# Block products of 256 columns, gate and up tiles by halves, and fewer adding DMAs in an fp32 encoder of two layers

## The chip, the cores and the metric

The kernel runs on one core of a Trainium2 chip. The metric is the device time of one execution in microseconds (us). Engines are named as in the profile: PE (TensorE, matmuls), PEld (its weight loads), DVE (VectorE), ACT (ScalarE), POOL (GpSimd) and SP (SyncE, here only a queue of DMAs).

## The reference

Input is one sequence of 512 rows and 1024 channels in float32. Two layers follow each other, each with a SwiGLU network, a mixer and a second SwiGLU network, and all of it in float32:

```
def _rmsnorm(x, gain):
    xf = x.astype(jnp.float32)
    y = xf * lax.rsqrt(jnp.mean(xf * xf, axis=-1, keepdims=True) + EPS)
    return (y * gain.astype(jnp.float32)).astype(x.dtype)
def _swiglu(h, w_gate, w_up, w_down):
    return (jax.nn.silu(h @ w_gate) * (h @ w_up)) @ w_down

# every layer:
#   x += 1/2 * SwiGLU(RMSNorm(x))                       1024 -> 2816 -> 1024
#   x += W_out [mixer_1 || mixer_2] (split of W_in RMSNorm(x))
#   x += 1/2 * SwiGLU(RMSNorm(x))
# even layer: Mamba-2 SSD heads || S5 complex-diagonal groups
# odd layer:  chunked band attention || multi-scale causal pooling
```

## The kernel before

**Stages.** The program runs six stages one after another: f0, even, f1 (layer 0) and f2, odd, f3 (layer 1). f0 to f3 are the SwiGLU networks, "even" and "odd" the mixers. x lies on the chip as eight tiles of 128 channels x 512 positions.

**Products.** An fp32 product is made of three matmuls (`mm3`): high part of the weights by high part of the data, high by low, low by high. So every weight unit (`raw`, 128 x 1024, by DMA) is split into `whl`: ACT casts it to the high part, DVE subtracts to get the low part (`split`). Units listed in `BY_DMA` take another way (`split_dma`): ACT writes the negated cast into the low part, a DMA of POOL adds the weights to it from memory, and ACT casts them into the high part; DVE does nothing.

**SwiGLU.** Gates and ups come in 11 pairs of 128-column tiles. The first pairs (`CLASSIC`: eight in f0, two in f1, f2, f3) are plain products of 512 columns (`proj_tile`); DVE multiplies them by the norm's factors rsB into `gs` and `us` (`evac`). The others, three pairs in f0 and nine in each of f1, f2, f3, gate and up each, 60 in all, go through `pair`: seven block products instead of eight, by sums of weights and of data (a scheme of Strassen's kind), into accumulators X, Y, Z on PE, which DVE adds up into `gs` or `us` (`plus`, `add`, `times`; p1 and p5 are small tiles). A `block` is four steps over 128 channels. A narrow block has three matmuls of 256 columns at each step. A wide one (three of the seven, where `WIDE`) puts the high weights against high and low data in one matmul of 512 columns, so that two halves of the accumulator must be added by DVE afterwards. `gate` takes silu of `gs` on ACT, multiplies by `us` on DVE, and splits the product into two `hg` tiles. Between the pairs stand units of the product with w_down (`out_unit`).

**Norms.** `norm` makes h from x as soon as a tile of x is final: ACT writes x times gain as the high part hg, DVE the low part. `norm_factors` squares each x tile on ACT (`sq`), DVE adds it to `acc`, PE multiplies by ones, DVE finds the inverse root (rqv, rqt, rqy), PE spreads it (ident, rqy) and ACT copies it to rsB.

**Even mixer.** Its small jobs are products with parameters of the S5 part (`prm`, eight matrices of 1 MB that a DMA loads), the products of the SSD part, the norm of its output (ysq) and transposes. Rows of the S5 part go through memory: us is stored as s5us and loaded again as hg, ys is stored as s5ys and loaded as yv.

**What sets the order.** PE, DVE and ACT run instructions in the order in which the builder writes them. A planner (`Clock`) holds an estimated time for each engine; the small jobs are generators that are advanced when the planner's clock says that their inputs are ready, `SLACK` later by stage, while the big products go on. It knows the Rings (`raw`, `whl`, `hg`), but not the waits for a buffer of an ordinary pool, such as `sq`:

```
                sq = self.rsp.tile([P, S], F32, tag="sq", name=self.n("sq"), bufs=2)
                nc.scalar.activation(out=sq, in_=x, func=AF.Square)
                yield from self.on("DVE", sq)
                nc.vector.tensor_tensor(out=acc, in0=acc, in1=sq, op=ALU.add)
```

Of the kernel before, what the change touches and what calls it, by code (L numbers as in the profile page):

```python
# [8 lines left out]
F32 = mybir.dt.float32  # L9
# [3 lines left out]
ALU = mybir.AluOpType  # L13
# [4 lines left out]
P = 128  # L18
# [23 lines left out]
CLASSIC = (2, 8)  # L42
LEAD = (0, 0)

WIDE = (True, True)

# [4 lines left out]
GUARD = {"f0": 2.5, "even": 1.5, "f1": 1.5, "f2": 1.5, "odd": 2.0, "f3": 1.5}  # L51
BY_DMA = {"wgu1": (1, 4), "wgu2": (1, 4), "wgu3": (1, 4), "wev": (13, 16), "wglu": (0, 2), "wevo": (0, 1), "wod": (8, 16), "wodo": (0, 1)}
LOADS = (1, 4)
LAG = 4
WARM = 12
SLACK = {"f0": 1.5, "even": 0.0, "f1": 0.0, "f2": 0.0, "odd": 0.4, "f3": 0.0}
PREP_SLACK = 4.0
# [53 lines left out]
class Clock:  # L111


    def __init__(self):
        self.t = dict.fromkeys(list(ENGINES.values()) + ["RING", "DMA"], 0.0)
        self.t["ACT"], self.t["RING"], self.t["DVE"], self.t["PE"] = 1.9, 0.65, 0.6, 0.95
        self.w, self.r, self.floor, self.stuck = {}, {}, 0.0, 0
        self.reads, self.writes, self.fine = {}, {}, True
        self.lanes, self.born = [0.0] * 8, {}
# [53 lines left out]
    def note(self, eng, op, args, kw):  # L173
# [14 lines left out]
        if dma and eng == "POOL":  # L188
            self.t["POOL"] = max(at, self.t["POOL"]) + 1.1
            end = max(self.t["DMA"], self.t["POOL"] + 1.0) + max(0.18, out.free_size() * out.partition_size() * 4 / 360e3)  # L190
            self.t["DMA"] = end
            end += 0.95
        elif dma:
            at = max(at, self.lanes.pop(0))
            self.t["RING"] = at + 0.48
            end = max(self.t["DMA"], at + 1.1) + max(0.06, out.free_size() * out.partition_size() * 4 / 360e3)
            self.t["DMA"] = end
            end += 1.06
            self.lanes.append(end)
        else:  # L200
            end = at + self.cost(eng, op, out, kw)
            if eng == "DVE" and self.fine:
                end += self.moved([ap for ap in ins if ap.free_size() > 1], out)
                if op == "reciprocal":
                    end += out.free_size() * 0.005
            self.t[eng] = end
# [61 lines left out]
class Builder:  # L268
# [27 lines left out]
    def phase(self, name):  # L296
        self.name = name
        self.clk.fine = name == "f0"
        self.backlog, self.guard, self.most = BACKLOG[name], GUARD[name], AHEAD[name]
# [352 lines left out]
    def norm_factors(self, h):  # L652
        nc = self.nc
        acc = None
        for k in range(KD):
# [4 lines left out]
            if acc is None:  # L660
                acc = self.rsp.tile([P, S], F32, tag="acc", name=self.n("acc"))
                nc.scalar.activation(out=acc, in_=x, func=AF.Square)
            else:
                sq = self.rsp.tile([P, S], F32, tag="sq", name=self.n("sq"), bufs=2)
                nc.scalar.activation(out=sq, in_=x, func=AF.Square)
                yield from self.on("DVE", sq)
                nc.vector.tensor_tensor(out=acc, in0=acc, in1=sq, op=ALU.add)
# [98 lines left out]
    def ffn(self, f, gi, then, prepare=None):  # L766
# [4 lines left out]
        with ExitStack() as st:  # L771
# [18 lines left out]
            for key in ffn_items(f):  # L790
# [11 lines left out]
                if key[0] == "wgu":  # L802
                    m, i = key[2:]
                    if (m % 2, i) == (0, 0):
                        t, done = {"gs": None, "us": None}, []
                    if (m, i) == (0, 0):
# [3 lines left out]
                    else:  # L810
                        w = self.unit(*key)
                        ps = self.proj_tile(w, h)
                        self.give(w)
                    self.add("evac", self.evac(ps, t, "us" if i else "gs", m % 2, done))
                    if (m % 2, i) == (1, 1):
                        self.add("gate", self.gate(t, g, m // 2, done, 0))
                        if m == NFF - 1:
                            self.give(*h)
                elif key[0] == "pair":
                    q, i = key[2:]  # L820
                    if i == 0:
                        t = {}
                    last = self.pair(w, t, "us" if i else "gs", pending)

                    def pending(last=last, t=t, q=q, i=i):
                        last()
                        if i == 0:
                            nc.scalar.activation(out=t["gs"], in_=t["gs"], func=AF.Silu)
                        else:
                            self.add("gate", self.gate(t, g, q, [1] * 4, 1))  # L830
                            if q == NFF // 2 - 1:
                                self.give(*self.N, *self.TS)
                else:
# [21 lines left out]
    def tail(self):  # L855
        self.final, self.xdone = True, [False] * KD
        if self.then is not None:
            self.start_norm(self.then)

    def ftile(self, tag):  # L860
        self.wait_room(tag, 1)
        return self.ft.tile([P, 2, S], F32, tag=tag, name=self.n(tag), bufs=1)

    def evac(self, ps, t, tag, m, done):
        while not self.scaled():
            yield
        while t[tag] is None and self.cnt.get(tag, 0):
            yield
        if t[tag] is None:
            self.cnt[tag] = 1  # L870
            t[tag] = self.ft.tile([P, 2, S], F32, tag=tag, name=self.n(tag), bufs=1)
        yield from self.on("DVE", ps, self.rsB)
        self.evac_rs(ps, t[tag][:, m])
        self.free(ps)
        done.append(1)

# [66 lines left out]

    def pair(self, w, t, tag, before):
        v = self.nc.vector
# [17 lines left out]
        if before:  # L963
            Z = self.main_ps()
            self.block(Z[:, hi], W4, 512, N[4:8], hi)
            before()
        t[tag] = dst = self.ftile(tag)
        Y = self.main_ps()
        self.block(Y, W3, 512, TA, 1, wide=wide)
        plus(dst[:, 0, hi], Y, p1)  # L970
        if not before:
# [4 lines left out]

        add(dst[:, 0, hi], Z[:, lo], dst[:, 0, hi])
        p5 = new("p5", 1)
        times(p5, Z[:, hi], hi)
        add(dst[:, 0, hi], dst[:, 0, hi], p5)  # L980
        self.block(X, W1, 512, N[4:8], lo, more=True)
        self.give(W1)
        times(dst[:, 0, lo], X[:, lo], lo)
        self.free(X)
        self.block(Y, W4, 0, TB, 0, more=True, wide=wide)
        self.give(W4)
        plus(dst[:, 1, hi], Y, p1)
# [1128 lines left out]
```

## Time and profile before

| | |
|---|---|
| three timed runs | 1807.51, 1810.75, 1813.69 us; median 1810.75 |
| profiled execution | 1812.46 us, of which the traced span is 1810.8 |
| granted TensorE clock, mean | 0.998 |
| PE busy | 1787.6 us (99%), 10082 matmuls |
| DVE busy | 1518.0 us (84%), 2902 instructions |
| ACT busy | 744.5 us (41%), 1032 |
| POOL busy | 33.9 us (2%) |
| DMA | 216.57 MB, mean 120 GB/s |
| the norms' products with ones, one at each stage's start | f0 21.2, even 384.9, f1 590.4, f2 937.9, odd 1284.3, f3 1466.3 us |

An engine's busy time is the union of its instructions' spans. A timeline row holds a start, a length, the engine, the line, the operation with its output and inputs (buffer numbers left out), the shape and how many instructions were merged into it. A row of waits holds who waited for whom, then the total, the times and the longest in us. All instructions are recorded at one line (L223), so groups go by tile names.

### The profile page before, as it was taken

To read this page: it belongs to the slowest core of one execution; us is meant where nothing else is said; L and a number is where in the kernel's file an instruction comes from. 1 tells how busy PE (TensorE), PEld (TensorE's weight loads), DVE (VectorE), ACT (ScalarE), POOL (GpSimd) and SP (SyncE) were. 2 spreads that over 40 slices of the span, in tenths; PEclk is the share of its full clock that TensorE was granted. 3 is DMA by queue.
4 is the path that set the end of the run, shared out by engine and by line. 5 is a ranking of instruction groups with operands and counts; after the bars stand their busy time and mean duration, and the time that the engine had idled before them with its cause. 6 is when DMAs were issued, how large, how long until landed. Compare 5 with 4: busy or idle time off the path is not lost.

```text
span 1810.8 us, 26209 instructions
## 1 busy us (share of the span) xinstructions
PE 1787.6 (99%) x10082; PEld 1536.4 (85%) x10082; DVE 1518.0 (84%) x2902; ACT 744.5 (41%) x1032; POOL 33.9 (2%) x53
## 2 busy tenths in 40 slices
PE   9999999999999999999999999999999999999999
PEld 7876888878778889998888999988888888999987
DVE  8989888778885899998779998987678679998984
ACT  4323433333584543333354333333466554333331
POOL 0000000000010000000010000000000010000000
PEclk9999999999999999999999999999999999999999
DMA  5346533336674533333343333333325452333332
GB/s 193 101 130 173 165 93 94 124 133 197 170 180 131 126 105 105 105 104 106 128 114 107 105 106 105 103 108 116 111 82 114 132 128 86 112 105 95 115 98 77
DMA packets 83341, 216.57 MB, mean 120 GB/s; under 512 B 18288, under 2 KB 30608, under 8 KB 82064
## 3 DMA queue, kind: packets, MB, share of 16 engines
q1 hardware_dynamic: 78032, 196.52, 33.9%
q0 software_dynamic: 5040, 18.35, 5.9%
q8 instruction: 79, 1.29, 0.3%
q14 instruction: 46, 0.38, 0.1%
q10 hardware_dynamic: 144, 0.02, 0.0%
HBM read 202.26 MB, written 12.60 MB: 119 GB/s over the span
## 4 chain that ended last, share of the span: by engine, by line
PE 75%; DVE 15%; DMA 5%; issue 2%; ACT 2%; SPq 1%; DVEq 0%; ACTq 0%
PE ps L223 75%; DVE whl L223 3%; DMA raw<-in_wgu_dram 2%; DVE hg L223 2%; DVE raw L223 2%; DVE us L223 1%; ACT whl L223 1%; DVE gs L223 1%; SPq L223 1%; DVE ct L223 1%; DVE ex L223 1%; DMA prm<-ct 1%; DVE g L223 0%; DMA prm<-prm 0%; DMA raw<-in_wev_dram 0%
## 5 line engine op out<-in xcount | busy, mean ns | idle before, releaser
L223 PE MATMUL ps<-hg,whl 128*128 128x512 f32 (+1 forms) x8400 | 1593.3, 350 | 5.4 <-DVE gs L223 2.5
L223 PEld LDWEIGHTS ps<-hg,whl 128*128 128x128 f32 x8400 | 1341.5, 189 | 210.9 <-issue 7.7
L223 ACT CAST whl<-raw 128x1024 fp32r<-128x1024 f32 x374 | 390.4, 1047 | 437.3 <-PE ps L223 306.6
L223 DVE TENSOR_TENSOR whl<-raw,whl 128x1024 fp32r<-128x1024 f32 x339 | 412.1, 1218 | 81.0 <-ACT whl L223 80.6
L223 ACT CAST hg<-us 128x512 fp32r<-128x512 f32 x88 | 52.7, 618 | 209.0 <-DVE us L223 208.9
L223 DVE TENSOR_TENSOR raw<-raw,raw 128x512 f32<-128x512 f32 (+1 forms) x212 | 131.0, 646 | 2.5
L223 ACT ACTIVATE gs<-gs 128x1024 f32<-128x1024 f32 x44 | 46.7, 1060 | 155.0 <-DVE gs L223 154.9
L223 DVE SCALAR_TENSOR_TENSOR x<-ps,x 128x512 f32<-128x512 f32 x128 | 83.1, 683 | 23.9 <-PE ps L223 23.9
L223 PE MATMUL ps<-hg,wh 128*128 128x512 f32 x480 | 94.2, 339 | 1.1 <-DVE gs L223 1.1
L223 PEld LDWEIGHTS ps<-hg,wh 128*128 128x128 f32 x480 | 77.3, 189 | 13.9 <-DVE gs L223 1.7
L223 DVE TENSOR_TENSOR us<-ps,us 128x256 f32<-128x256 f32 x150 | 63.5, 424 | 22.2 <-PE ps L223 17.8
L223 DVE TENSOR_TENSOR raw<-raw 128x512 f32<-128x512 f32 (+1 forms) x92 | 54.5, 592 | 18.9 <-DMA raw<-in_wgu_dram 18.8
L223 DVE TENSOR_TENSOR gs<-ps,gs 128x256 f32<-128x256 f32 x150 | 63.6, 424 | 6.6 <-PE ps L223 1.0
L223 DVE TENSOR_TENSOR hg<-us,hg 128x512 fp32r<-128x512 f32 x88 | 58.4, 684 | 2.7 <-ACT hg L223 2.7
L223 DVE TENSOR_TENSOR us<-gs,us 128x1024 f32<-128x1024 f32 x44 | 53.7, 1220 | 0.4
L223 DVE TENSOR_TENSOR us<-ps,p 128x256 f32<-128x256 f32 x90 | 37.8, 419 | 16.1 <-PE ps L223 15.4
L223 DVE TENSOR_TENSOR p<-ps,rsB 128x256 f32<-128x256 f32 x120 | 49.9, 416 | 1.7 <-PE ps L223 1.7
L223 ACT ACTIVATE hg<-x,gains 128x512 fp32r<-128x512 f32 x48 | 33.5, 718 | 34.6 <-DVE x L223 32.1
L223 DVE TENSOR_TENSOR gs<-ps,p 128x256 f32<-128x256 f32 x90 | 37.8, 420 | 8.1 <-PE ps L223 6.3
L223 DVE TENSOR_TENSOR wh<-raw,wh 128x512 fp32r<-128x512 f32 x60 | 41.0, 684 | 0.0
L223 ACT ACTIVATE whl<-raw 128x1024 fp32r<-128x1024 f32 x35 | 36.9, 1056 | 8.1 <-PE ps L223 5.1
L223 DVE SCALAR_TENSOR_TENSOR hg<-x,gains,hg 128x512 fp32r<-128x512 f32 x48 | 35.3, 745 | 5.7 <-ACT hg L223 5.7
(258 smaller groups left out, 1084.2 us busy)
## 6 DMA issues: line engine op xcount, KB each, us to landing
raw<-in_wgu_dram SPq DMA_DIRECT2D x176, 512.0 KB, 3.5
raw<-in_wdn_dram SPq DMA_DIRECT2D x88, 512.0 KB, 4.1
whl<-in_wgu_dram POOLq DMA_DIRECT2D x18, 512.0 KB, 6.3
raw<-in_wev_dram SPq DMA_DIRECT2D x16, 512.0 KB, 4.2
prm<-prm SPq DMA_DIRECT2D x8, 1024.0 KB, 6.9
raw<-in_wod_dram SPq DMA_DIRECT2D x12, 512.0 KB, 3.5
raw<-in_wevo_dram SPq DMA_DIRECT2D x8, 512.0 KB, 6.4
raw<-in_wodo_dram SPq DMA_DIRECT2D x8, 512.0 KB, 6.4
```

The costliest lines, as they stand in the source:

```text
L223: r = f(*args, **kw)
```

## The change

1. `WIDE` becomes false for all stages: every block is narrow, and `plus` is one add.
2. `gs` and `us` were one tile of 128 x 2 x 512 each, of one buffer. They are now tiles of 128 x 512, three buffers of gs and two of us (`HALVES`). Silu, product and split are done for each half, as soon as it is complete (`ready`).
3. `BY_DMA` of the gate and up weights in f1, f2, f3 covers two pairs of 128-column tiles instead of three: m = 2 and 3, no longer 1. Six units fewer go by POOL's adding DMA (18 before, 12 after), and those are split by DVE.
4. `SLACK` of the even mixer is 0.5 where it was 0.
5. The planner reckons POOL's DMAs in f1, f2, f3 at 160 GB/s where it reckoned 360.
6. The tile `sq` has one buffer where it had two.

```diff
-
-WIDE = (True, True)
+HALVES = {"gs": 3, "us": 2}
+
+WIDE = (False, False)
...
-BY_DMA = {"wgu1": (1, 4), "wgu2": (1, 4), "wgu3": (1, 4), "wev": (13, 16), "wglu": (0, 2), "wevo": (0, 1), "wod": (8, 16), "wodo": (0, 1)}
+BY_DMA = {"wgu1": (2, 4), "wgu2": (2, 4), "wgu3": (2, 4), "wev": (13, 16), "wglu": (0, 2), "wevo": (0, 1), "wod": (8, 16), "wodo": (0, 1)}
-SLACK = {"f0": 1.5, "even": 0.0, "f1": 0.0, "f2": 0.0, "odd": 0.4, "f3": 0.0}
+SLACK = {"f0": 1.5, "even": 0.5, "f1": 0.0, "f2": 0.0, "odd": 0.4, "f3": 0.0}
...
-            end = max(self.t["DMA"], self.t["POOL"] + 1.0) + max(0.18, out.free_size() * out.partition_size() * 4 / 360e3)
+            end = max(self.t["DMA"], self.t["POOL"] + 1.0) + max(0.18, out.free_size() * out.partition_size() * 4 / (160e3 if self.ffn else 360e3))
...
-                sq = self.rsp.tile([P, S], F32, tag="sq", name=self.n("sq"), bufs=2)
+                sq = self.rsp.tile([P, S], F32, tag="sq", name=self.n("sq"), bufs=1)
...
                 elif key[0] == "pair":
                     q, i = key[2:]
                     if i == 0:
                         t = {}
-                    last = self.pair(w, t, "us" if i else "gs", pending)
-
-                    def pending(last=last, t=t, q=q, i=i):
+                    def ready(m, t=t, q=q, i=i):
+                        if i == 0:
+                            nc.scalar.activation(out=t["gs", m], in_=t["gs", m], func=AF.Silu)
+                        else:
+                            self.add("gate", self.gate(t, g, q, m, False))
+
+                    last = self.pair(w, t, "us" if i else "gs", pending, ready)
+
+                    def pending(last=last, q=q, i=i):
                         last()
-                        if i == 0:
-                            nc.scalar.activation(out=t["gs"], in_=t["gs"], func=AF.Silu)
-                        else:
-                            self.add("gate", self.gate(t, g, q, [1] * 4, 1))
-                            if q == NFF // 2 - 1:
-                                self.give(*self.N, *self.TS)
+                        if (q, i) == (NFF // 2 - 1, 1):
+                            self.give(*self.N, *self.TS)
...
     def ftile(self, tag):
-        self.wait_room(tag, 1)
-        return self.ft.tile([P, 2, S], F32, tag=tag, name=self.n(tag), bufs=1)
+        self.wait_room(tag, HALVES[tag])
+        return self.ft.tile([P, S], F32, tag=tag, name=self.n(tag), bufs=HALVES[tag])
...
-        t[tag] = dst = self.ftile(tag)
+        t[tag, 0] = d0 = self.ftile(tag)
         Y = self.main_ps()
         self.block(Y, W3, 512, TA, 1, wide=wide)
-        plus(dst[:, 0, hi], Y, p1)
+        plus(d0[:, hi], Y, p1)
         if not before:
             Z = self.main_ps()
             self.block(Z[:, hi], W4, 512, N[4:8], hi)
         self.block(Z, W3, 0, TA, 0)
         self.give(W3)
 
-        add(dst[:, 0, hi], Z[:, lo], dst[:, 0, hi])
+        add(d0[:, hi], Z[:, lo], d0[:, hi])
         p5 = new("p5", 1)
         times(p5, Z[:, hi], hi)
-        add(dst[:, 0, hi], dst[:, 0, hi], p5)
+        add(d0[:, hi], d0[:, hi], p5)
         self.block(X, W1, 512, N[4:8], lo, more=True)
         self.give(W1)
-        times(dst[:, 0, lo], X[:, lo], lo)
+        times(d0[:, lo], X[:, lo], lo)
         self.free(X)
+        ready(0)
+        t[tag, 1] = d1 = self.ftile(tag)
         self.block(Y, W4, 0, TB, 0, more=True, wide=wide)
         self.give(W4)
-        plus(dst[:, 1, hi], Y, p1)
-        add(dst[:, 1, hi], Z[:, lo], dst[:, 1, hi])
+        plus(d1[:, hi], Y, p1)
+        add(d1[:, hi], Z[:, lo], d1[:, hi])
         self.free(Z)
 
         def last():
             self.block(Y, W2, 0, TB, 1, more=True, wide=wide)
             self.give(W2)
-            plus(dst[:, 1, lo], Y, p1)
+            plus(d1[:, lo], Y, p1)
             self.free(Y)
+            ready(1)
         return last
...
-    def gate(self, t, g, q, ready, done):
+    def gate(self, t, g, q, m, silu):
         nc = self.nc
-        while len(ready) < 4:
-            yield
-        gs, us = t["gs"], t["us"]
-        if done < 1:
+        gs, us = t["gs", m], t["us", m]
+        if silu:
             yield from self.on("ACT", gs)
             nc.scalar.activation(out=gs, in_=gs, func=AF.Silu)
-        if done < 2:
-            yield from self.on("DVE", gs, us)
-            nc.vector.tensor_tensor(out=us, in0=gs, in1=us, op=ALU.mult)
+        yield from self.on("DVE", gs, us)
+        nc.vector.tensor_tensor(out=us, in0=gs, in1=us, op=ALU.mult)
         self.leave("gs")
-        for i in range(2):
-            o = yield from self.grab("hg")
-            yield from self.split_steps(us[:, i], o)
-            g[2 * q + i] = o
+        o = yield from self.grab("hg")
+        yield from self.split_steps(us, o)
+        g[2 * q + m] = o
         self.leave("us")
```

**What moves.** PE, a wide block of a pair in f0, before (Y, with the data sums hg and the weights whl; a step's three rows of work in two matmuls):

```order
L223 MATMUL ps_2573<-hg_2036,whl_2472 128x512 [waits Activation_49]
L223 MATMUL ps_2573<-hg_2036,whl_2472 128x256
L223 MATMUL ps_2573<-hg_2090,whl_2472 128x512
L223 MATMUL ps_2573<-hg_2090,whl_2472 128x256
L223 MATMUL ps_2573<-hg_2157,whl_2472 128x512
L223 MATMUL ps_2573<-hg_2157,whl_2472 128x256
L223 MATMUL ps_2573<-hg_2257,whl_2472 128x512
L223 MATMUL ps_2573<-hg_2257,whl_2472 128x256
```

and after:

```order
L224 MATMUL ps_2616<-hg_2066,whl_2507 128x256 [waits Activation_49]
L224 MATMUL ps_2616<-hg_2066,whl_2507 128x256 x2
L224 MATMUL ps_2616<-hg_2137,whl_2507 128x256 x3
L224 MATMUL ps_2616<-hg_2214,whl_2507 128x256 x3
L224 MATMUL ps_2616<-hg_2297,whl_2507 128x256 x3
```

Eight matmuls, four of them of 512 columns, are now twelve of 256; the places of the blocks in PE's order stay as they were.

ACT at the norm of f1, before (sq is the square of an x tile, hg the high part of x times gain, whl a weight unit; DVE_49 is a wait for DVE, DMAHW for a load):

```order
L223 ACTIVATE sq_5346<-x_123 128x512 [waits Activation_49]
L223 ACTIVATE sq_5376<-x_125 128x512 [waits DVE_49]
L223 ACTIVATE whl_5378<-raw_5257 128x1024 [waits DMAHW1_49]
L223 CAST whl_5378<-raw_5257 128x1024
L223 ACTIVATE hg_5374<-x_127,gains 128x512 [waits DVE_49]
L223 ACTIVATE whl_5395<-raw_5286 128x1024 [waits DMAHW2_49]
L223 CAST whl_5395<-raw_5286 128x1024
L223 ACTIVATE sq_5412<-x_127 128x512 [waits DVE_49]
L223 ACTIVATE whl_5417<-raw_5317 128x1024 [waits DMAHW3_49,PE_49]
```

and after:

```order
L224 ACTIVATE sq_5446<-x_123 128x512 [waits DVE_49]
L224 ACTIVATE sq_5476<-x_125 128x512 [waits DVE_49]
L224 CAST whl_5478<-raw_5357 128x1024 [waits DMAHW5_49,DMAHW1_49]
L224 ACTIVATE hg_5474<-x_127,gains 128x512
L224 CAST whl_5490<-raw_5386 128x1024 [waits DMAHW2_49]
L224 ACTIVATE whl_5502<-raw_5417 128x1024 [waits DMAHW3_49,PE_49]
L224 CAST whl_5502<-raw_5417 128x1024
L224 ACTIVATE sq_5516<-x_127 128x512 [waits DVE_49,Activation_49]
```

The squares sq_5446 (of x_123), sq_5476 (of x_125) and sq_5516 (of x_127) now wait for DVE's add of the square before, since they use its buffer. Two units (m = 1) that were negated and cast are only cast here, which leaves their subtraction to DVE, and the last square stands behind a third unit's negation and cast.

DVE at the same place, before:

```order
L223 TENSOR_TENSOR acc_5186<-acc_5186,sq_5333 128x512 [waits Activation_49]
L223 TENSOR_TENSOR x_127<-ps_5228,x_127 128x512 [waits PE_49]
L223 SCALAR_TENSOR_TENSOR hg_5340<-x_125,gains,hg_5340 128x512 [waits Activation_49]
L223 TENSOR_TENSOR acc_5186<-acc_5186,sq_5346 128x512 [waits DVE_49,Activation_49]
L223 TENSOR_TENSOR acc_5186<-acc_5186,sq_5376 128x512 [waits DVE_49,Activation_49]
L223 SCALAR_TENSOR_TENSOR hg_5374<-x_127,gains,hg_5374 128x512 [waits Activation_49]
L223 TENSOR_TENSOR acc_5186<-acc_5186,sq_5412 128x512 [waits DVE_49,Activation_49]
```

and after:

```order
L224 TENSOR_TENSOR acc_5286<-acc_5286,sq_5433 128x512 [waits Activation_49]
L224 TENSOR_TENSOR x_127<-ps_5328,x_127 128x512 [waits PE_49]
L224 SCALAR_TENSOR_TENSOR hg_5440<-x_125,gains,hg_5440 128x512 [waits Activation_49]
L224 TENSOR_TENSOR acc_5286<-acc_5286,sq_5446 128x512 [waits Activation_49]
L224 TENSOR_TENSOR whl_5478<-raw_5357,whl_5478 128x1024 [waits DMAHW2_49,DMAHW4_49,DMAHW1_49,Activation_49]
L224 TENSOR_TENSOR whl_5490<-raw_5386,whl_5490 128x1024 [waits DMAHW2_49,Activation_49]
L224 SCALAR_TENSOR_TENSOR hg_5474<-x_127,gains,hg_5474 128x512 [waits DVE_49]
L224 TENSOR_TENSOR acc_5286<-acc_5286,sq_5476 128x512 [waits DVE_49]
L224 TENSOR_TENSOR acc_5286<-acc_5286,sq_5516 128x512 [waits Activation_49]
```

The two subtractions (whl_5478, whl_5490) have come in ahead of the low half hg_5474 of the last x tile and of the last two adds.

SP's queue in the even mixer, before (s5us and s5ys are the rows that go through memory, yv and hg their loads, prm the parameters):

```order
L223 DMA s5ys_3999<-ys_3942 16x8x64 x8
L223 DMA s5us_3969<-us_3960 128x512
L223 DMA prm_4011<-prm_144 128x2048
L223 DMA prm_4077<-prm_145 128x2048
L223 DMA raw_4082<-in_wev_dram 128x1024
L223 DMA s5ys_4084<-ys_3990 16x8x64 x8
L223 DMA yv_4093<-s5ys_3999 128x512
L223 DMA hg_4101<-s5us_3969 16x16x64 x8
```

and after:

```order
L224 DMA s5ys_4090<-ys_4067 16x8x64 x8
L224 DMA s5us_4048<-us_4039 128x512
L224 DMA prm_4101<-prm_143 128x2048
L224 DMA prm_4121<-prm_144 128x2048
L224 DMA raw_4145<-in_wev_dram 128x1024
L224 DMA yv_4171<-s5ys_4090 128x512
L224 DMA hg_4177<-s5us_4048 16x16x64 x8
L224 DMA raw_4215<-in_wev_dram 128x1024
L224 DMA prm_4228<-prm_145 128x2048
L224 DMA s5ys_4233<-ys_4119 16x8x64 x8
```

The load of hg from s5us stood behind the second set of stores s5ys; it now stands ahead of it, behind the load of yv.

More of the change, by code (lines that the diff above doesn't have):

```diff
@@ L117, in __init__ @@
         self.w, self.r, self.floor, self.stuck = {}, {}, 0.0, 0
-        self.reads, self.writes, self.fine = {}, {}, True
+        self.reads, self.writes, self.fine, self.ffn = {}, {}, True, False
         self.lanes, self.born = [0.0] * 8, {}
@@ L297, in phase @@
         self.name = name
-        self.clk.fine = name == "f0"
+        self.clk.fine, self.clk.ffn = name == "f0", name in ("f1", "f2", "f3")
         self.backlog, self.guard, self.most = BACKLOG[name], GUARD[name], AHEAD[name]
@@ L804, in ffn @@
                     if (m % 2, i) == (0, 0):
-                        t, done = {"gs": None, "us": None}, []
+                        t = {}
                     if (m, i) == (0, 0):
@@ L813, in ffn @@
                         self.give(w)
[L814 to L818, printed above, removed]
+                    self.add("evac", self.evac(ps, t, "us" if i else "gs", m % 2, g, m // 2))
+                    if (m, i) == (NFF - 1, 1):
+                        self.give(*h)
                 elif key[0] == "pair":
@@ L860, in ftile, with evac @@
     def ftile(self, tag):
-        self.wait_room(tag, 1)
-        return self.ft.tile([P, 2, S], F32, tag=tag, name=self.n(tag), bufs=1)
-    def evac(self, ps, t, tag, m, done):
+        self.wait_room(tag, HALVES[tag])
+        return self.ft.tile([P, S], F32, tag=tag, name=self.n(tag), bufs=HALVES[tag])
+    def evac(self, ps, t, tag, m, g, q):
         while not self.scaled():
             yield
-        while t[tag] is None and self.cnt.get(tag, 0):
-            yield
-        if t[tag] is None:
-            self.cnt[tag] = 1
-            t[tag] = self.ft.tile([P, 2, S], F32, tag=tag, name=self.n(tag), bufs=1)
+        yield from self.room(tag, HALVES[tag])
+        o = self.ft.tile([P, S], F32, tag=tag, name=self.n(tag), bufs=HALVES[tag])
         yield from self.on("DVE", ps, self.rsB)
-        self.evac_rs(ps, t[tag][:, m])
+        self.evac_rs(ps, o)
         self.free(ps)
-        done.append(1)
+        t[tag, m] = o
+        if tag == "us":
+            self.add("gate", self.gate(t, g, q, m, True))
     def normed(self, r, k, h, gi, late):
@@ L940, in block, with pair @@
             self.tick()
-    def pair(self, w, t, tag, before):
+    def pair(self, w, t, tag, before, ready):
         v = self.nc.vector
@@ L993, in last @@
             self.give(W2)
-            plus(dst[:, 1, lo], Y, p1)
+            plus(d1[:, lo], Y, p1)
             self.free(Y)
+            ready(1)
         return last
-    def gate(self, t, g, q, ready, done):
+    def gate(self, t, g, q, m, silu):
         nc = self.nc
-        while len(ready) < 4:
-            yield
-        gs, us = t["gs"], t["us"]
-        if done < 1:
+        gs, us = t["gs", m], t["us", m]
+        if silu:
             yield from self.on("ACT", gs)
             nc.scalar.activation(out=gs, in_=gs, func=AF.Silu)
-        if done < 2:
-            yield from self.on("DVE", gs, us)
-            nc.vector.tensor_tensor(out=us, in0=gs, in1=us, op=ALU.mult)
+        yield from self.on("DVE", gs, us)
+        nc.vector.tensor_tensor(out=us, in0=gs, in1=us, op=ALU.mult)
         self.leave("gs")
-        for i in range(2):
-            o = yield from self.grab("hg")
-            yield from self.split_steps(us[:, i], o)
-            g[2 * q + i] = o
+        o = yield from self.grab("hg")
+        yield from self.split_steps(us, o)
+        g[2 * q + m] = o
         self.leave("us")
```

## The prediction, made before the changed kernel ran

> **What bounds the kernel now.** I read the page first: busy shares, then the clock row, then the list of PE's waits.
>
> ```profile
> PE 1787.6 (99%) x10082; PEld 1536.4 (85%) x10082; DVE 1518.0 (84%) x2902; ACT 744.5 (41%) x1032; POOL 33.9 (2%) x53
> PE 75%; DVE 15%; DMA 5%; issue 2%; ACT 2%; SPq 1%; DVEq 0%; ACTq 0%
> ```
>
> PE is busy 1787.6 of 1810.8 us. Only two things can move the time: the 1787.6 themselves, and the 23.2 us in which PE stands. The second line, the chain that ended last, says the same: three quarters PE. DVE has 16% to spare on the average, so work taken from DVE is worth only what PE waits for it.
>
> ```profile
> PE ps L223 <- DVE gs L223: 3.6, 7, 0.9
> PE ps L223 <- DVE bt L223: 2.7, 4, 1.2
> PE ps L223 <- DMA prm<-prm: 2.3, 1, 2.3
> PE ps L223 <- DMA hg<-s5us: 2.0, 1, 2.0
> PE ps L223 <- DVE hg L223: 1.6, 2, 1.2
> PE ps L223 <- ACT bl L223: 1.3, 1, 1.3
> PE ps L223 <- DVE ysq L223: 1.2, 1, 1.2
> PE ps L223 <- DVE cr L223: 0.9, 1, 0.9
> ```
>
> These are PE's waits (total, times, longest). The gs row is the first pair of f1, f2, f3; bt and bl are preparations in f0; prm, s5us, one hg of 1.2, ysq and cr are the even mixer. None is in the steady pairs.
>
> **Narrow blocks.** A pair's three wide blocks (4 matmuls of 512 columns and 4 of 256) become 12 matmuls of 256. The timeline of f2 has one of each, a wide one and then the next pair's first narrow one (start, length with the drain of the last matmul):
>
> ```profile
> 1104.57 1.56 PE L223 MATMUL ps<-hg,wh 128*128 128x512 f32 x8
> 1105.97 1.60 PE L223 MATMUL ps<-hg,whl 128*128 128x256 f32 x12
> ```
>
> 1.60 against 1.56 is 0.04 us a block; the wide one's 8 matmuls take 1.40 to the next start. There are 60 pairs, so 180 blocks: 180 x 0.04 = **+7.2 us**, all of it on PE. The two rows bound it closely, 6 to 8. The Trainium skill's "TensorE: Matmul & The Clock Gate", section "Back-to-back issue gap", has N/2.4 + 2.5 ns for a matmul of N columns, by which a split matmul costs only 2.5 ns more: 4 x 2.5 = 10 ns a block and +1.8 us in all. The trace's 40 ns disagree, and I keep them.
>
> **One add less, halves, fewer adding DMAs.**
>
> ```profile
> L223 DVE TENSOR_TENSOR us<-ps,us 128x256 f32<-128x256 f32 x150 | 63.5, 424 | 22.2 <-PE ps L223 17.8
> L223 DVE TENSOR_TENSOR us<-gs,us 128x1024 f32<-128x1024 f32 x44 | 53.7, 1220 | 0.4
> L223 DVE TENSOR_TENSOR acc<-acc,sq 128x512 f32<-128x512 f32 x42 | 28.8, 686 | 5.9 <-ACT sq L223 5.0
> L223 DVE TENSOR_TENSOR whl<-raw,whl 128x1024 fp32r<-128x1024 f32 x339 | 412.1, 1218 | 81.0 <-ACT whl L223 80.6
> ```
>
> 180 adds at 0.424 leave DVE (-76 us). Products by halves cost 88 x 0.686 - 44 x 1.220 = +7 us (taking the 512-column add's duration for a 512-column product), and six weight units that a POOL DMA finished are now split by DVE: 6 x 1.218 = +7. All this lies beside PE: the steady pairs wait for nothing, so I count 0. If that cover went, DVE being 84% busy, it would be a gain of DVE time, not a loss. ACT's silus by halves are 44 more small instructions on an engine at 41%: 0. POOL and its queue lose six DMAs: 0. The planner's price for these DMAs moves loads, not engine work.
>
> Where DVE is late, it matters: the first pairs of f1 to f3 stall for 3.5 us of the gs row. DVE there has one add less before the accumulators come free, and a gs half frees sooner. Between 0 and 3.5 gained, perhaps 1.5 lost by the added split; I take **-1.5**. The f0 waits (bt 2.7, bl 1.3, 4.0 together) meet the same relief, and the small products they feed sit two to four places later in PE's order: between 0 and -4, I take **-2**.
>
> **One sq buffer.** A norm squares x on ACT (sq) and adds on DVE (acc). With two buffers ACT ran one square ahead; with one, each square waits for the add of the last, and everything behind it in ACT's order waits too: casts of weights and the high halves of hg. The start, before (ACT, then DVE, then PE):
>
> ```profile
> 8.63 1.14 ACT L223 ACTIVATE sq<-x 128x512 f32<-128x512 f32 x2
> 9.68 1.03 ACT L223 CAST whl<-raw 128x1024 fp32r<-128x1024 f32 x1
> 10.04 0.68 DVE L223 TENSOR_TENSOR acc<-acc,sq 128x512 f32<-128x512 f32 x1
> 10.74 1.23 DVE L223 TENSOR_TENSOR whl<-raw,whl 128x1024 fp32r<-128x1024 f32 x1
> 18.00 2.28 DVE L223 TENSOR_TENSOR acc<-acc,sq 128x512 f32<-128x512 f32 x3
> 21.24 0.95 PE L223 MATMUL ps<-ones,acc 128*128 128x1 f32 x8
> ```
>
> The second square ran at 9.15; it now waits for the add that ends at 10.72, so the cast behind it goes from 9.68 to 11.3, its split from 10.74 to 12.35, and PE's second weight unit starts 1.6 later. Following the same durations on, with the third cast (18.8), its split (19.85 to 21.1), the low half of the last hg (21.7) and then three add, square, add turns of 1.3 each, the last add ends at 25.0 where it was 20.3, and PE's product with ones, at 21.24 before, starts at 25.05: **+3.8** (bounds 1.6, the first link alone, and 5).
>
> At the start of f1 (ACT, DVE, PE), and the last add and PE's product in f2 and f3:
>
> ```profile
> 581.85 0.62 ACT L223 ACTIVATE sq<-x 128x512 f32<-128x512 f32 x1
> 583.38 1.26 ACT L223 ACTIVATE sq<-x 128x512 f32<-128x512 f32 x2
> 588.94 0.62 ACT L223 ACTIVATE sq<-x 128x512 f32<-128x512 f32 x1
> 583.29 0.68 DVE L223 TENSOR_TENSOR acc<-acc,sq 128x512 f32<-128x512 f32 x1
> 585.15 1.48 DVE L223 TENSOR_TENSOR acc<-acc,sq 128x512 f32<-128x512 f32 x2
> 589.60 0.69 DVE L223 TENSOR_TENSOR acc<-acc,sq 128x512 f32<-128x512 f32 x1 [1.67 <-ACT sq L223]
> 590.38 1.02 PE L223 MATMUL ps<-ones,acc 128*128 128x1 f32 x8
> ...
> 936.72 0.69 DVE L223 TENSOR_TENSOR acc<-acc,sq 128x512 f32<-128x512 f32 x1 [1.66 <-ACT sq L223]
> 937.93 0.95 PE L223 MATMUL ps<-ones,acc 128*128 128x1 f32 x8
> ...
> 1465.51 0.69 DVE L223 TENSOR_TENSOR acc<-acc,sq 128x512 f32<-128x512 f32 x1 [1.67 <-ACT sq L223]
> 1466.35 1.02 PE L223 MATMUL ps<-ones,acc 128*128 128x1 f32 x8
> ```
>
> The product with ones follows the last add by 0.1 in f1. Now the sixth square waits for the add ending 583.97 (start 584.0, was 583.38), the seventh for the add ending 585.83 (start 585.9). Behind it stand a cast (to 587.45), the last hg's high half, a cast (to 589.05), a negation and a cast (to 591). On DVE the two added splits stand ahead of the seventh add (to 590.3), then the hg low half, and the add ends at 591.5; only then the eighth square, and its add ends at 592.95. PE, which stands in order behind its product, loses 593.0 - 590.4 = 2.6. f3 repeats f1 (2.5); f2 ends at 938.8 against 937.93 (0.9). Together **+6.0** (bounds 0, if the splits were ahead of time, and 9). In the even and odd norms ACT has no casts between, so the waits add 0.15 each: 0.
>
> **The even mixer.** Of these three stretches (the third number from the end is the granted clock) two show a clock below 1, and the queue of SP shows why PE waited for s5us:
>
> ```profile
> 454.00:462.00 8.00, 5.97 (x61) 4.96 (x60) 6.11 (x14) 3.27 (x5) 0.00 (x0) 0.79 0.91 249
> 474.00:482.00 8.00, 5.70 (x51) 5.01 (x50) 5.77 (x12) 2.36 (x5) 0.00 (x0) 1.00 0.61 197
> 540.00:547.00 7.00, 5.85 (x25) 4.79 (x25) 4.01 (x14) 2.20 (x3) 0.83 (x1) 0.76 0.99 232
> 440.64 8.62 SPq L223 DMA_DIRECT2D s5ys<-ys  x8
> 449.78 4.02 SPq L223 DMA_DIRECT2D hg<-s5us  x8
> ```
>
> A granted clock of 0.79 over 8 us and 0.76 over 7 is half clock for 3.4 us: 1.7 us lost each, beside the stall that precedes it (2.03 at 455; 1.2 and 1.15 at 533 and 540). The eight s5us loads stood behind eight s5ys stores that held the queue 8.6 us; they now stand ahead of them, so this stall and its half clock go: -3.7. What the queue does later is the stores and the loads of yv, which have slack: 0. The prm stall (2.3): the load of the seventh matrix is some places earlier in the queue, though PE's use is too, by four groups of three matmuls of 0.68 us each; -1.5. The cr stall (0.9): PE's product sits two such groups (1.4 us) later; -0.9. The ysq and hg stalls (2.3, and 1.7 of clock): the products sit three groups (2 us) later; -1.9. Sum **-8**; bounds 0 (other jobs become late) and -12 (all of it: 2.0 + 2.3 + 0.9 + 2.4 + 1.1 in small ones + 3.4).
>
> **New half clocks.** PE gets gaps of 1 to 2.6 us at four norms. Before, the 2.0 was followed by half clock and the 2.3 for prm, in the stretch from 474, was not; I take one of four, **+1.7** (0 to 6.8). The skill's same page, "HAM oscillation", asks for idle gaps over about 3.4 us, by which this term would be 0; the 2.0 us gap above disagrees.
>
> **Sum.** 7.2 - 1.5 - 2 + 3.8 + 6.0 - 8 + 1.7 = +7.2. The profiled execution took 1812.46 (span 1810.8), 1.7 above the median 1810.75. So 1819.7 for it, and **1818** for the median.
>
> **Rivals.**
> 1. The squares' waits are hidden (DVE, lighter, has done the splits early): without 3.8 + 6.0 + 1.7 the time is 1810.75 - 4.3 = 1806.5. For it: nothing else uses the result earlier. Against: 0.1 us of slack in f1.
> 2. Faster: DVE's 76 us are the real limit behind PE's waits, and every wait for DVE and for the even jobs goes, those of the squares included: 7.2 - 12 - 3.5 - 4 = -12.3, **1798.5**. It decides once the last add of f1 ends by about 590.4 on the old scale. For it: DVE stands behind five of the eight rows of waits. Against: around the norms DVE idles before the acc adds.
> 3. The even mixer gains nothing, since later small jobs make others late: 1826.
> 4. The page's 2.5 ns rule holds: 1818 - 5.4 = 1812.6.
>
> **How the numbers follow.** A measurement here tells about 0.3% (5.4 us) from no change. My forecast holds 0.45 (own range 1813 to 1822; three quarters of it is slower by more than 0.3%), rival 1 0.20 (two fifths faster), rival 2 0.15, rival 3 0.15, rival 4 0.05. Faster 0.08 + 0.14 = 0.22; slower 0.34 + 0.15 = 0.49; same 0.29. The range 1804 to 1826 leaves out most of rival 2 and half of rival 3.
>
> **What would show it.** PE's matmuls of 512 columns fall by 720 and those of 256 rise by 1440, with PE's busy time near 1795; no wide rows of 8 in the pairs. The waits list names DVE acc for ACT's sq with some 10 us where the trace had 2.5, and PE waits for DVE at the product with ones in f0, f1, f3 for 2 to 3 us. The s5us row is gone from PE's waits, the clock at that place is 1. I am wrong if PE's busy time is unchanged, if ones,acc shows no wait, or if stalls appear inside steady pairs.

## The result, and the profile after

The changed kernel takes 1832.18 us (median of four runs, 1831.23 to 1834.04) against 1811.57 in the same job: a ratio of 1.0121, 95% interval 1.0105 to 1.0138. It is 20.6 us slower where 7 were forecast, and lies above the range. The profiled execution took 1831.23, its span is 1829.5, 18.7 over the span before.

First the busy shares of the changed kernel:

```profile
PE 1801.8 (98%) x10802; PEld 1581.1 (86%) x10802; DVE 1455.3 (80%) x2773; ACT 750.2 (41%) x1070; POOL 28.8 (2%) x47
```

DVE lost 63 us of work and PE gained 14 us of busy time. The 720 matmuls more are those of the narrow blocks; they can't explain 14 us, as will be seen. Next, PE's waits (total, times, longest):

```profile
PE ps L224 <- DVE acc L224: 6.8, 4, 2.6
PE ps L224 <- DVE s_sc L224: 2.9, 2, 2.4
PE ps L224 <- DVE hg L224: 2.2, 2, 2.0
PE ps L224 <- DVE g L224: 1.8, 1, 1.8
PE ps L224 <- ACT whl L224: 1.4, 1, 1.4
PE ps L224 <- ACT ssb L224: 1.3, 1, 1.3
PE ps L224 <- DVE bt L224: 1.3, 2, 0.9
PE ps L224 <- DVE gs L224: 0.8, 2, 0.6
...
ACT sq L224 <- DVE acc L224: 30.4, 25, 2.6
```

The row at the top was not there before: PE's products with ones wait for the last add of a norm. The last row is its source: ACT's squares wait 30.4 us for DVE's adds where they waited 2.5 (the prediction expected some 10). The waits for gs fell from 3.6 to 0.8. In the even mixer s5us and prm have gone, but s_sc and ssb have come. The row of g is a preparation in f0, at 164.5 us; bl has gone there and bt is half of what it was.

The place in f1 that the prediction worked out, PE's rows, then ACT's, then DVE's:

```profile
597.69 1.84 PE L224 MATMUL ps<-ones,acc 128*128 128x1 f32 x8 [2.63 <-DVE acc L224]
599.39 5.23 PE L224 MATMUL ps<-hg,whl 128*128 128x512 f32 x12
...
590.44 0.63 ACT L224 ACTIVATE sq<-x 128x512 f32<-128x512 f32 x1 [1.23 <-DVE acc L224]
596.19 0.63 ACT L224 ACTIVATE sq<-x 128x512 f32<-128x512 f32 x1 [0.72 <-DVE acc L224]
...
592.04 1.23 DVE L224 TENSOR_TENSOR whl<-raw,whl 128x1024 fp32r<-128x1024 f32 x1 [1.64 <-ACT whl L224]
593.61 1.23 DVE L224 TENSOR_TENSOR whl<-raw,whl 128x1024 fp32r<-128x1024 f32 x1 [0.34 <-ACT whl L224]
596.85 0.69 DVE L224 TENSOR_TENSOR acc<-acc,sq 128x512 f32<-128x512 f32 x1 [0.76 <-ACT sq L224]
```

The gap of 2.63 us is there as forecast. But look at the second row: twelve matmuls of 512 columns take 5.23 us, where the same twelve took 3.01 before. The windows say why (the third number from the end is the granted clock):

```profile
597.40:604.10 6.70, 6.41 (x19) 5.47 (x20) 1.94 (x12) 0.00 (x0) 0.00 (x0) 0.50 0.30 56
1481.50:1488.20 6.70, 6.33 (x19) 5.40 (x20) 2.01 (x12) 0.00 (x0) 0.00 (x0) 0.50 0.34 66
```

That is half clock for 6.8 us behind the norm of f1, and again behind that of f3. Matmuls at half clock are busy for longer (5.23 us against 3.01), so PE's 14 us more are in good part this: ahead of its last 2 us this execution has 27.3 us at half clock, the one before had 6.8.

The starts of the products with ones cut the span into stages. Lengths in us from one to the next (f0 to the even norm, and so on), in the profiled executions:

| | to f0 | f0 | even | f1 | f2 | odd | f3 |
|---|---|---|---|---|---|---|---|
| before | 21.24 | 363.68 | 205.46 | 347.55 | 346.34 | 182.08 | 344.40 |
| changed | 25.06 | 364.84 | 207.78 | 351.92 | 345.78 | 186.47 | 347.65 |
| difference | +3.82 | +1.17 | +2.32 | +4.37 | -0.56 | +4.40 | +3.25 |

A wait at the norm of f1 is at the end of "even", its half clock at the start of "f1"; in the same way f3's are in "odd" and "f3".

### The profile page after: what moved, and what is told of

The parts are those of the page before. It is cut to its first block, busy times and chain, and to the rows that moved or that the text cites. A ratio compares the mean times of both kernels' runs of the same rounds, so it can differ in the third digit from the quotient of the medians.

```text
span 1829.5 us, 27498 instructions
## 1 busy us (share of the span) xinstructions
PE 1801.8 (98%) x10802; PEld 1581.1 (86%) x10802; DVE 1455.3 (80%) x2773; ACT 750.2 (41%) x1070; POOL 28.8 (2%) x47
## 3 DMA queue, kind: packets, MB, share of 16 engines
q8 instruction: 85, 1.39, 0.3%
## 4 chain that ended last, share of the span: by engine, by line
PE 74%; DVE 18%; DMA 3%; ACT 3%; issue 2%; SPq 0%; ACTq 0%; DVEq 0%
PE ps L224 74%; DVE whl L224 4%; DVE raw L224 3%; DVE hg L224 2%; ACT whl L224 1%; DVE us L224 1%; DVE gs L224 1%; DVE acc L224 1%; DVE x L224 1%; DVE s_t L224 1%; DMA yv<-s5ys 1%; DMA raw<-in_wgu_dram 1%; DVE ct L224 1%; DVE ex L224 1%; DMA ssb<-acsd 0%
## 5 line engine op out<-in xcount | busy, mean ns | idle before, releaser
L224 PE MATMUL ps<-hg,whl 128*128 128x256 f32 (+1 forms) x8880 | 1601.5, 340 | 6.2 <-DVE hg L224 2.0
L224 PEld LDWEIGHTS ps<-hg,whl 128*128 128x128 f32 x8880 | 1370.7, 191 | 188.1 <-issue 4.7
L224 DVE TENSOR_TENSOR whl<-raw,whl 128x1024 fp32r<-128x1024 f32 x345 | 419.0, 1218 | 129.7 <-ACT whl L224 129.6
L224 ACT ACTIVATE gs<-gs 128x512 f32<-128x512 f32 x88 | 55.5, 631 | 168.2 <-DVE gs L224 168.2
L224 PEld LDWEIGHTS ps<-hg,wh 128*128 128x128 f32 x720 | 93.9, 191 | 4.4
L224 PE MATMUL ps<-hg,wh 128*128 128x256 f32 x720 | 96.0, 283 | 0.0
L224 DVE TENSOR_TENSOR us<-gs,us 128x512 f32<-128x512 f32 x88 | 60.1, 683 | 3.9 <-ACT gs L224 3.6
L224 DVE TENSOR_TENSOR us<-ps,us 128x256 f32<-128x256 f32 x60 | 25.5, 424 | 32.8 <-PE ps L224 31.4
L224 ACT ACTIVATE sq<-x 128x512 f32<-128x512 f32 x42 | 26.3, 626 | 30.5 <-DVE acc L224 30.4
L224 ACT CAST wh<-raw 128x512 fp32r<-128x512 f32 x60 | 36.9, 615 | 0.0
```

The costliest lines, as they stand in the source:

```text
L224: r = f(*args, **kw)
```

## Experiments

### The sq buffer, taken from the kernel before and given back to the changed one

```diff
# b_sq1: the kernel before
-                sq = self.rsp.tile([P, S], F32, tag="sq", name=self.n("sq"), bufs=2)
+                sq = self.rsp.tile([P, S], F32, tag="sq", name=self.n("sq"), bufs=1)
# a_sq2: the changed kernel
-                sq = self.rsp.tile([P, S], F32, tag="sq", name=self.n("sq"), bufs=1)
+                sq = self.rsp.tile([P, S], F32, tag="sq", name=self.n("sq"), bufs=2)
-HALVES = {"gs": 3, "us": 2}
+HALVES = {"gs": 2, "us": 2}
```

> The kernel before with one buffer for sq instead of two; the order of instructions on PE, DVE and ACT stays word for word. Theory A (the one buffer is the main cost): the first product with ones moves from 21.2 to about 25.0 us (+3.8), that of f1 and f3 waits about 1.8 us each for the last add, f2 hardly; with half clocks behind these gaps +8 to +14 us over before, 1819 to 1825. Rival B (the narrow blocks are the main cost): at most +3.

> The changed kernel with two buffers for sq again; the room comes from gs, which has two half buffers instead of three. The order on PE, DVE and ACT stays the same but for buffer numbers. Theory A: the waits of ACT for acc go back to about 2.5 us, PE's waits for acc (6.8 us) vanish, the start is 3.8 us earlier, and the half clocks after the norms of f1 and f3 (together 4.6 us) go: -12 to -15 us, 1817 to 1820. Rival B: not more than -3, above 1829. If gs with two halves mattered, waits of PE for gs would come up in the pairs.

b_sq1 took 1821.98 us, ratio 1.0069 (1.0051 to 1.0087); a_sq2 took 1813.44, ratio 1.0015 (1.0006 to 1.0024), 18.7 below the changed kernel. Theory A came out in both directions; a_sq2 gained even more than it foresaw (1817 to 1820). In a_sq2 the norm of f1 reads as it did before:

```profile
591.44 1.02 PE L224 MATMUL ps<-ones,acc 128*128 128x1 f32 x8
592.33 3.01 PE L224 MATMUL ps<-hg,whl 128*128 128x512 f32 x12
...
ACT sq L224 <- DVE acc L224: 2.5, 2, 2.1
```

So taking one buffer of 2 KB in each partition away is worth 18.7 of the 20.6 us in the changed kernel, though rival B's narrow blocks, halves, DMAs and order all stayed. In b_sq1 it costs 11: the waits are shorter there (1.80 at f1 and at f3), without the two subtractions in the chain:

```profile
PE ps L223 <- DVE gs L223: 4.4, 9, 0.8
PE ps L223 <- DVE acc L223: 4.3, 4, 1.8
PE ps L223 <- DVE hg L223: 3.3, 4, 1.4
```

No wait for gs came up in a_sq2's pairs: the third half buffer of gs, for which the second sq was given up, did nothing that can be seen.

### The gap filled

```diff
# a_fill: the changed kernel
         pss = self.side_ps()
+        for _ in range({"f1": 11, "f3": 11, "f2": 3}.get(self.name, 0)):
+            self.tc.nc.tensor.matmul(out=pss, lhsT=h[0][:, 0, 0:P], rhs=h[0][:, 0], start=True, stop=True)
         for j in range(4):
```

> The changed kernel (one sq buffer) with idle matmuls of 512 columns put ahead of the products with ones at the norms of f1 (11), f2 (3) and f3 (11), whose results are overwritten; 11 take 2.5 us, so they fill the time in which PE waited for the last add and add almost none of their own. Theory A (the half clock of 6.8 us behind these norms comes from the gap of 2.6 us): the half clock at about 597 and 1481 us is gone, 4 to 5 us faster than the changed kernel, 1826 to 1828. Rival D (the half clock comes from the transfers or from other work there): no change, 1830 or more.

1825.12 us, ratio 1.0083 (1.0067 to 1.0099): about 7 us faster than the changed kernel by doing more. The timeline at the same place, and the windows of both norms:

```profile
595.70 2.65 PE L672 MATMUL ps<-hg 128*128 128x512 f32 x11
598.40 1.05 PE L224 MATMUL ps<-ones,acc 128*128 128x1 f32 x8
599.32 3.01 PE L224 MATMUL ps<-hg,whl 128*128 128x512 f32 x12
...
598.40:605.10 6.70, 6.70 (x37) 5.84 (x38) 3.03 (x13) 1.84 (x3) 0.01 (x1) 1.00 0.27 54
1479.50:1486.20 6.70, 6.70 (x38) 5.81 (x39) 3.09 (x13) 1.93 (x3) 0.09 (x1) 1.00 0.26 50
```

The product with ones still starts just behind the last add of acc (all of this stands 0.8 later in this run), but PE comes to it busy, and the clock stays at 1. "f1" went from +4.37 to +1.24, "f3" from +3.25 to +0.24: 6.1 us of the loss was the clock, not the wait. Rival D falls: with the same transfers and the same work around it, only the gap was taken away. The timed runs agree: their granted clock is 0.995 to 0.997, where the changed kernel's four have 0.992 or 0.993.

### Narrow blocks, and halves

```diff
# b_narrow: the kernel before                # a_sq2_wide: a_sq2
-WIDE = (True, True)                         -WIDE = (False, False)
+WIDE = (False, False)                       +WIDE = (True, True)
# c_halves: b_narrow, with gs and us by halves as in the change (two buffers each), nothing else of it
```

> The kernel before with narrow blocks alone; the even mixer keeps the order of before, three products later. Theory A: 180 blocks at 0.028 to 0.04 us more, 5 to 7 us, less 1 to 3 for the add less at the first pairs: +3 to +6. By a rule of 2.5 ns for each added matmul: +2 and less the same relief, 0. Rival B: +12 or more.

> The changed kernel with two sq buffers (1813.4 us) and wide blocks again, so 180 adds of DVE more. Theory A: the narrow blocks cost 0.028 to 0.04 us each and their relief of DVE is worth little once gs and us come by halves: 5 to 7 us faster, 1806 to 1809. Rival F (with the adds back, DVE is late again at the first pairs): 1811 or more, with 3 us of waits for gs.

> The kernel before with narrow blocks (1821.8 us by itself) and gs and us by halves, two buffers each; adding DMAs, SLACK and the planner's price as before. Theory G (with narrow blocks, the halves free accumulators earlier at the first pairs of f1, f2, f3): the 8.2 us of PE's waits for gs fall to about 1 and the time to 1809 to 1812. Rival H (the relief in the changed kernel came from fewer adding DMAs or the planner's new price): 1817 or more.

b_narrow took 1821.75 us, ratio 1.0058 (1.0043 to 1.0073), 10.9 over before: more than theory A, a little less than B. a_sq2_wide took 1814.13, ratio 1.0019 (1.0009 to 1.0028), no faster than a_sq2: theory A's 5 to 7 us did not come. c_halves took 1815.16, ratio 1.0029 (1.0019 to 1.0039), between what theory G and rival H expected. The first rows of PE's waits, of b_narrow and of c_halves, with one of b_narrow's waits in f2 (DVE, then PE):

```profile
PE ps L223 <- DVE gs L223: 8.2, 7, 1.9
PE ps L223 <- DMA hg<-s5us: 3.0, 2, 1.5
...
PE ps L224 <- DVE hg L224: 5.5, 5, 2.0
PE ps L224 <- DVE g L224: 2.1, 1, 2.1
...
1006.21 1.22 DVE L223 TENSOR_TENSOR us<-gs,us 128x1024 f32<-128x1024 f32 x1
1007.54 0.42 DVE L223 TENSOR_TENSOR gs<-ps,p 128x256 f32<-128x256 f32 x1
1008.01 8.72 PE L223 MATMUL ps<-hg,whl 128*128 128x256 f32 x36 [1.93 <-DVE gs L223]
```

With narrow blocks and whole tiles PE waits 8.2 us for DVE's adds into gs, where wide blocks had 3.6: on DVE the product of gs and us, 1.22 us in one piece, stands ahead of the adds that free the accumulators. With halves these waits are off the list, and 6.6 us between the medians with them; whether by the smaller pieces or by the second buffer is not separated. A part comes back as waits for hg at the first pairs (1.0, 2.0 and 0.9 us in f1, f2, f3; the row of g is in f0). With a_sq2's other changes these are gone too. Theory G holds for gs, but the rest of the relief came with the fewer adding DMAs or the planner's new price; no run separates those two.

Against wide blocks in the same frame the narrow ones cost little: in a_sq2_wide f1, f2 and f3 are 1.76, 0.32 and 0.17 us shorter than in a_sq2, 2.25 together. The total shows nothing of it because "even" was 4.8 us longer there in the profiled execution, with a wait of 3.3 for ssb and half clock from 495 to 502. With SLACK 0 the pair a_sq2_slack0 and a_sq2_wide_slack0 (below) says the same: 2.1 us shorter in the three stages, and 2.2 longer in the odd mixer, with half clock at 1292 us.

### SLACK of the even mixer

```diff
# a_slack0: the changed kernel; a_sq2_slack0: a_sq2; a_sq2_wide_slack0: a_sq2_wide. b_slack: the kernel before, the other way round
-SLACK = {"f0": 1.5, "even": 0.5, "f1": 0.0, "f2": 0.0, "odd": 0.4, "f3": 0.0}
+SLACK = {"f0": 1.5, "even": 0.0, "f1": 0.0, "f2": 0.0, "odd": 0.4, "f3": 0.0}
```

> The changed kernel with the even mixer's SLACK at 0 again, which gives back the old order of that stage. Theory A (the new order only swaps one wait for memory against another): within 3 us of the changed kernel, with the s5us stall of about 2 us back and those for s_sc, ssb and hg (5.7 us) gone. Rival C (the later small jobs cost): 5 us faster or more.

> The changed kernel with two sq buffers (1813.4 us) and the even mixer's SLACK at 0. Theory A (the new order of the even mixer swaps the wait for s5us against waits for yv): 1812 to 1815. Rival C (SLACK 0.5 costs by itself what the run with one sq buffer gained, 5 us): 1809 or less. Rival E (the new order brings what the prediction said, 8 us): 1820 or more.

> As the run before it and SLACK of the even mixer 0. Theory A: 1806 to 1809, the same as with SLACK 0.5; if the two effects add and rival C holds, 1804.

> The kernel before with SLACK 0.5 in the even mixer alone; its products then stand in the order that the changed kernel has. Theory A now (the new order swaps the wait for s5us against waits for yv, and brings one more half clock): 3 to 5 us slower, 1813.5 to 1816. The prediction's term: 8 us faster.

| | SLACK 0 | SLACK 0.5 | costs |
|---|---|---|---|
| kernel before | 1810.3 | 1815.32 (ratio 1.0028, 1.0016 to 1.0040) | 5.0 |
| changed kernel | 1826.70 (1.0088, 1.0071 to 1.0105) | 1832.18 | 5.5 |
| changed, two sq buffers | 1809.08 (0.9993, 0.9984 to 1.0002) | 1813.44 | 4.4 |
| the same, wide blocks | 1810.45 (1.0001, 0.9992 to 1.0010) | 1814.13 | 3.7 |

Four pairs agree: the new order of the small jobs costs 3.7 to 5.5 us. The expectation for a_slack0 (within 3 us) was wrong and rival C right, as b_slack on the kernel before confirms; a_sq2_wide_slack0 reached neither of its expectations. Where it begins shows in PE, ACT, DVE and SP of the changed kernel around the second load of yv; below the dots are SP and ACT of the kernel before:

```profile
475.49 0.43 PE L224 MATMUL ps<-s_sc,prm 128*128 128x63 f32 x2 [2.44 <-DVE s_sc L224]
472.03 0.63 ACT L224 ACTIVATE g<-yv 128x512 f32<-128x512 f32 x1 [5.69 <-DMA yv<-s5ys]
472.69 0.69 DVE L224 SCALAR_TENSOR_TENSOR g<-g,yv 128x512 f32<-128x512 f32 x1 [2.50 <-ACT g L224]
468.21 0.33 SPq L224 DMA_DIRECT2D yv<-s5ys  x1
470.00:484.00 14.00, 11.56 (x75) 9.84 (x75) 11.11 (x28) 6.85 (x12) 1.00 (x1) 0.88 0.91 259
...
454.34 1.10 SPq L223 DMA_DIRECT2D yv<-s5ys  x1
458.86 0.63 ACT L223 ACTIVATE g<-yv 128x512 f32<-128x512 f32 x1 [1.43 <-DMA yv<-s5ys]
```

The load of yv goes out at 468.21, some 9 us later in its stage than before, and ACT's g, the first user, runs at 472.03. DVE's g waits for ACT, the scan's products s_sc stand behind it in DVE's order, and PE waits 2.44 for them; half clock follows (0.88 over 14 us). The wait for s5us (2.0) was exchanged for one for yv (2.4). The other kernels with SLACK 0.5 have the same wait (PE for s_sc, 1.6 to 2.3 us at once); in those with SLACK 0 it is at most 0.5.

The waits alone don't make 4 to 5 us: PE stands 8.7 us in this stage in the kernel before and 8.5 in b_slack. Most of it is clock. Over the timed runs the mean granted clock is 0.9985 before and 0.9962 in b_slack; (1 - clock) x time, an estimate of what half clock cost, is 2.7 and 7.0 us. In the three other pairs it rises by 4.2, 2.7 and 2.6.

### Versions that could beat both

```diff
# c_narrow_fill: a_sq2_slack0; c_wide_fill: the same and WIDE = (True, False), wide in f1, f2, f3
         pss = self.side_ps()
+        if self.chunked == 2:
+            for _ in range(5):
+                self.tc.nc.tensor.matmul(out=pss[:, 0:P], lhsT=self.ones, rhs=self.ones, start=True, stop=True)
```

> The changed kernel with two sq buffers and SLACK 0 (1809.1 us), and five idle matmuls of 128 columns ahead of the second product of ones with ysq, where PE waited 1.2 us and half clock followed. If the gap brings the half clock: 1.5 us less, 1807 to 1808. If not: 1809.

> As the run before it, with wide blocks in f1, f2, f3. The three stages were 2.2 us shorter with wide blocks in the pair of runs with two sq buffers: 1805 to 1806.5. If a half clock comes up elsewhere (the odd mixer had one in one of the runs): 1807 to 1809.

c_narrow_fill took 1810.08 us, ratio 0.9999 (0.9991 to 1.0008), no gain: the half clock behind ysq is gone from its profiled run, but there is one at 9 and one at 1292 us, and over its timed runs the mean clock is 0.9980 where a_sq2_slack0 had 0.9984. c_wide_fill took 1806.89, ratio 0.9984 (0.9975 to 0.9992), the fastest kernel here, 3.4 us below the kernel before; its profiled run has no half clock ahead of the last 0.6 us, and f1 to f3 are 2.8 us shorter than before. That run was lucky with the clock: the mean over its timed runs is 0.9986, as in the kernel before, so the gain lies in the stages. PE and the other engines in its profiled run:

```profile
PE 1785.7 (99%) x10164; PEld 1537.6 (85%) x10164; DVE 1517.7 (84%) x2934; ACT 746.8 (41%) x1070; POOL 28.8 (2%) x47
```

## Why the prediction was wrong

The direction was right, the size was not. Rivals 1 and 2 fell with the row of 6.8 us for acc. Two steps failed in the main: the even mixer, which had no slack where the prediction gave it some, and the price of the half clock that follows a gap. By the prediction's own steps:

**Narrow blocks, +7.2: too large.** The two rows of one block each gave 0.040 us. Start to start, over the steady pairs of f2, a wide step takes 235 + 118 ns and a narrow one 3 x 120, 7 ns more, so 0.028 a block and 5.0 us in all. From a_sq2_wide to a_sq2 PE's busy time in f1 to f3 grows by 3.6 us (0.022 a block), and its waits there shrink by 1.3, so that 2.25 is left in the stages' lengths. The 2.5 ns of the Trainium skill ("TensorE: Matmul & The Clock Gate", "Back-to-back issue gap") would be 0.010 a block; its gaps for 256 and 512 columns (109 and 216 ns, given there for isolated matmuls) are not this trace's (120 and 227).

**Halves, 0: wrong with narrow blocks.** "The steady pairs wait for nothing, so I count 0" was read from a trace with wide blocks. Taking the wide blocks alone away brought PE's waits for gs to 8.2 us, and halves took them off. First pairs and narrow blocks together were +5.7 in the sum; in a_sq2 f1, f2 and f3 differ from before by +0.25, -0.81 and -0.16.

**One sq buffer, +3.8 and +6.0: right as waits.** The product with ones was worked out for 25.05 and stands at 25.06; that it agrees to a hundredth is luck, since it stands at 25.3 to 25.4 in the three other runs with one buffer. The waits at f1, f2 and f3 were put at 2.6, 0.9 and 2.5 and are 2.63, 0.85 and 2.63. Following one chain row by row through three engines' orders was the part that held. What the waits bring after them, the next term, was not.

**New half clocks, +1.7: the term that was mis-sized.** It was "one of four". Two of the four gaps brought half clock of 6.8 us, twice the 3.4 seen before, and filling them gave back 6.1 us. A third, of 1.39 at the start, was followed by half clock at 13.7 us, but PE waited for acc later there, so it cost nothing more (b_sq1, without that half clock, reached the product with ones no earlier). One more stood in the odd mixer at 1307 us, where fifteen products take 5.30 us that took 3.71 before (1.6 us):

```profile
1306.27 5.30 PE L224 MATMUL ps<-whl,hg 128*128 128x512 f32 x15 [0.27 <-DVE rqv L224]
...
1295.04 3.71 PE L223 MATMUL ps<-whl,hg 128*128 128x512 f32 x15 [0.27 <-DVE rqv L223]
```

**The even mixer, -8: wrong in sign.** The step that failed is "what the queue does later is the stores and the loads of yv, which have slack: 0". They had none. The first effect came as forecast, the stall for s5us is gone; I had not asked what the queue would be late with next. Alone the move costs 5.0 us on the kernel before, 4.3 of it clock by the estimate above: the half clock behind s5us (1.7 us) was counted as saved, and half clock came back elsewhere in the stage. Rival 3 (no gain, 1826) was near; with half clocks of 6.1 + 1.6 in place of 1.7 it gives 1832, the measured time, but by luck, since it keeps the 7.2 for the narrow blocks and leaves out what SLACK costs.

**f0, -2: wrong, small.** The waits for bt and bl fell from 4.0 to 1.3 us, but the one for g (1.8) came. The stage is 0.8 longer in a_sq2, where half clock follows that wait at 161 us, and 0.2 shorter in a_sq2_slack0, where it doesn't.

Summed again for the profiled executions (+18.7): waits at four norms 3.8 + 2.6 + 0.9 + 2.6 = 9.9, half clocks behind f1's and f3's 6.1 and in the odd mixer 1.6, together 17.6. All the rest of the change, narrow blocks, halves, fewer DMAs and the even mixer, comes to 1.1. That rest is a balance: with SLACK 0 and two sq buffers (a_sq2_slack0) the even mixer is 3.6 us shorter than before, and SLACK 0.5 gives this back.

The clock is nearly the whole miss. By (1 - clock) x time, half clock cost the changed kernel 13.3 us in its timed runs and the kernel before 2.2 to 2.7 in the later jobs: about 11 of the 20.6 us, where the sum took new half clocks for +1.7 and counted the old one behind s5us as saved. The other terms together came out near their forecast because their errors, too much for the narrow blocks and too little for the even mixer, had opposite signs; that is luck.

## What to carry to other kernels

A buffer count on a tile off the critical path can be the dearest line of a change, when the engine that waits for it has casts for the critical engine queued behind. Price a gap on PE with what follows it: here 2.6 us of waiting cost 5.7. And when a transfer is moved forward in a queue, look up the first user of each transfer that it passes. Compare the mean granted clock of the timed runs, not of the profiled one alone, before a difference of a few us is put down to waits.

## What the hardware showed

The granted clock falls to half in pieces of 3.41 us, one or two in a row (477.9 to 481.3, 597.4 to 604.2). The Trainium skill ("TensorE: Matmul & The Clock Gate", "What's actually happening") describes a free-running window of about 3.4 us, and the lengths agree with it. Its rule of thumb, in "HAM oscillation", asks for no idle gaps over about 3.4 us; here the measurement decides otherwise: 2.63 us sufficed at f1 and f3, and at the start two gaps of 1.39 and 0.53 within 3 us did. Nor is a long gap needed at all: at 1307 us half clock came after 16 small products (hm, sqk, 1.84 us) and a gap of 0.27, in some kernels and not in others with the same work there.

The traces show a window of this length, and that its place against the work is chance. In each of the 14 runs' traces the changes of the clock lie whole multiples of 3.413 us apart (in the changed kernel 58.03 us, 17 of them, from 539.3 to 597.4; c_wide_fill has only one change), and this grid lies elsewhere against the span's start from run to run. When each trace is cut into pieces by its own grid, each of the 20 pieces in which the profile counts PE busy for less than half of the time was followed by half clock, and none of the 17 with 52 to 61% (2 of the 6 between). First two with half clock behind them, from the changed kernel and from the kernel before, then the two pieces over which the 2.30 us for prm fell (PE busy, then the granted clock of the piece itself):

```profile
593.95:597.36 3.41, 1.11 (x5) 1.00 0.36 44
454.30:457.71 3.41, 1.38 (x17) 1.00 0.99 232
...
474.78:478.19 3.41, 2.70 (x21) 1.00 0.88 305
478.19:481.60 3.41, 1.82 (x21) 1.00 0.21 55
```

So a gap of 2.63 us is enough where it falls into one piece, and one of 2.30 was not where it fell across two. Above 61% it stays open: half clock followed some pieces with small products, which the profile counts as busy (66 and 92%), and not others.
